# Closing norms with factor and scaled sum in PSUM, and six plain tiles at the head of the second MLP

## The chip, the cores and the metric

The kernel runs on one core of a Trainium2 chip. A core has TensorE (PE, matmuls into PSUM), VectorE (DVE), ScalarE (ACT), GpSimd (POOL) and SyncE (SP), which issues the DMAs here. The metric is the device time of one execution in microseconds. Before the change it is 2682.29 us, the median of 3 runs (2672.32 to 2683.67).

## What is computed

One inference step of a decoder trunk of two layers, for a prompt of 1024 tokens and a sample group of 32, with shared weights, in fp32. Layer 0 mixes by differential attention and a convolution, layer 1 by an S5 state space. Each mixer is followed by an MLP with squared ReLU, and every one of these four stages has an RMS norm before it and one behind it, ahead of the residual sum:

```python
def rms_norm(x, g, eps=RMS_EPS):
    xf = x.astype(jnp.float32)
    y = xf * lax.rsqrt(jnp.mean(xf * xf, axis=-1, keepdims=True) + eps)
    return (y * g.astype(jnp.float32)).astype(x.dtype)

def sq_relu_mlp(xn, w_up, w_down):
    return jnp.square(jax.nn.relu(xn @ w_up)) @ w_down

# D_MODEL = 1024, D_FF = 4096, SEQ = 1024, DEC_BATCH * DEC_SEQ = 32
for l in range(DEPTH):                     # DEPTH = 2
    ...                                    # l = 0: attention + conv mixer, l = 1: S5 mixer
    hp = hp + rms_norm(mix, g_mix_post[l])
    ...
    hp = hp + rms_norm(sq_relu_mlp(rms_norm(hp, g_ffn_pre[l]), w_ffn_up[l], w_ffn_down[l]), g_ffn_post[l])
    hs = hs + rms_norm(sq_relu_mlp(rms_norm(hs, g_ffn_pre[l]), w_ffn_up[l], w_ffn_down[l]), g_ffn_post[l])
```

## The kernel before

The 1056 tokens lie along the columns, in three chunks of 352 (`NCH`, `CH`); the 1024 features are eight tiles of 128 partitions (`KT`). Each operand of a large matmul is split into a high and a low part, and a product is three matmuls, hi x hi, hi x lo, lo x hi (`mm3`, L203 to L205). A plain group, one weight tile against one chunk, is therefore 24 matmuls of 352 columns in one tile of PSUM. PSUM tiles come from one pool of eight with a single tag (`PS`); SBUF tiles of 128x352 come from another (`H`). A weight tile of 128x1024 is loaded (`wraw`), cast on ScalarE (`whi`, L196), and its rest taken on VectorE (`wlo`, L197).

A stage ends in `posts`: per chunk, the products of the last weight tiles are added up in `y`, squared (ScalarE, L300) and summed over the eight tiles into `ssq`, seven additions of which the last (`YV`) is on VectorE and the others on POOL (L301). `colsum` turns `ssq` by one matmul (`cs`, L183) into column sums, and `factor_of` (L175 to L178, ScalarE and VectorE in turn) into the factor `rpost`. Then `post` goes over the eight tiles: L323 scales `y` in place, L324 subtracts it from the residual `hres` (the tile holds the negative sum; four of eight on POOL, `HP`), `split` makes the next stage's operand (ACT L229, VectorE L230), ScalarE squares, and POOL adds these squares into `ssq2` (L333), from which the next stage's factor comes in the same way. While one chunk's `post` runs, TensorE does the products of the next chunk.

There are four such closings. Three of them (mixer 0, first MLP, mixer 1) lead into a next stage; the fourth, of the second MLP, into the outputs, its last chunk in `end`. The second MLP (`ffn_q`) does its first four units of 128 hidden rows as plain groups (`NB`, `up`), three chunks each, one hidden tile `hp` at a time going out to DRAM (`hid`), and the other 28 in 14 pairs: seven products of 24 matmuls with 264 columns for two units, a Strassen-like scheme. Its operands are sums of halves of the input (`sums`, on VectorE and ScalarE, L460 to L469, in the background) and sums of quarters of two weight tiles (`quads`, tiles `op`, from `wq`), which VectorE and ScalarE split as well (L226, L227). L646 takes a plain group's result out of PSUM, with the ReLU and the factor of the norm.

The order of the instructions on each engine is set by a scheduling framework when the kernel is built: the Python code is written in generators whose yields give rough costs, and the framework places the emitted instructions. Within the engines' order, waits are semaphores. SP's queue keeps the program's order, and a DMA whose source isn't ready holds up what stands behind it.

Of the kernel before, what the change touches and what calls it, by code (L numbers as in the profile page):

```python
# [13 lines left out]
ALU = mybir.AluOpType  # L14
# [8 lines left out]
CH = 352  # L23
NCH = T // CH
# [4 lines left out]
NB = 4  # L29
PW, RT = 7.0, 0.9  # L30
XA = ()
TR = 1.0
HP, YV, PE, EP = (0, 2), (7,), 14.0, ((1, 1), (2, 1))


def chunk(c):
    return slice(c * CH, (c + 1) * CH)
# [13 lines left out]
class Step:  # L51
# [261 lines left out]
    def post(self, y, c, s, gk, l, h, nxt):  # L313

        nc = self.nc
        yield PW
        r = self.H("rpost")
        self.factor_of(r, self.colsum(s, CH))
        s2 = self.H("ssq2") if nxt is not None else None
        yield 0.5  # L320
        for k in range(KT):
            yc = y[k][:, chunk(c)]
            nc.vector.scalar_tensor_tensor(yc, yc, self.g(gk, l, k), r, op0=ALU.mult, op1=ALU.mult)  # L323
            (nc.gpsimd if k % 4 in HP else nc.vector).tensor_sub(yc, h[k], yc)  # L324
            if nxt is not None:
                X, rn, rs, g2, l2 = nxt[:5]
                self.split(X[k][0][:, chunk(c)], X[k][1][:, chunk(c)], yc, self.g(g2, l2, k))
                if k == 0:
                    nc.scalar.activation(s2, yc, AF.Square)
                else:  # L330
                    q = self.H("sq")
                    nc.scalar.activation(q, yc, AF.Square)
                    nc.gpsimd.tensor_add(s2, s2, q)  # L333
            yield 1.0
        if nxt is None:
            yield from self.store(y, c)
            return
        self.fins.append((s2, nxt[1][:, chunk(c)]))
        if c == NCH - 1:
            for k in range(KT):  # L340
                self.dma(nxt[2][k], y[k])
            if nxt[5]:
                self.T = [[None] * 4 for _ in range(4)]
                self.bg_add(self.sums(list(y), g2, l2, self.T), TR)

# [280 lines left out]
    def ffn_q(self, l, X, r, res, nxt, early=None, beside=None):  # L626


        nc = self.nc
# [3 lines left out]
        raws = {}  # L633
        slot = [None, 3]

        def raw(u):
            if u < 32:
                raws[u] = [self.S("wq") for _ in range(2)]
                for i in range(2):
                    self.dma(raws[u][i][:, :1024].rearrange("p (k m) -> p k m", k=4),  # L640
                             up_w[512 * i:512 * i + 512, u * P:(u + 2) * P].rearrange("(k p) m -> p k m", p=P))

        def up(u, c):
            pt = self.block(w[u], slice(0, P), X, c)
            t1 = self.H("t")
            nc.vector.scalar_tensor_tensor(t1, pt, 0.0, r[:, chunk(c)], op0=ALU.max, op1=ALU.mult)  # L646
            if slot[1] == 3:
                slot[:] = self.S("hp"), 0
            h = slot[0][:, chunk(slot[1])]
            slot[1] += 1  # L650
            nc.scalar.activation(h, t1, AF.Square)
            self.dma(hd[u][:, chunk(c)], h)
            self.pump(3.7)
# [4 lines left out]
        ops = []  # L658
        for c in range(NCH):
            self.chunk_ready(c)  # L660
            if c == NCH - 1:
                raw(NB)
                steps = self.quads(raws[NB])
            for u in range(NB):
                up(u, c)
                if c == NCH - 1:
                    del w[u]
                    if u:
                        ops.append(next(steps))
        slot[0] = None  # L670
        self.drain()

# [1 line left out]
        for k in range(4):  # L674
            z = self.T[2][k][:, B:]
# [22 lines left out]
        def ahead():  # L698
            prep(0)
            yield  # L700
            for u in range(4):
                if u == 2:
                    prep(1)
                hload(u)
                yield

        first, more = True, None
        for u in range(NB, 32, 2):
            hu, hv = self.S("hu"), self.S("hv")
            nxt_ops = []  # L710
            if u == 30:
                more = ahead()
            else:
                raw(u + 2)
            nsteps = None
            for p in range(7):
                while len(ops) <= p:
                    ops.append(next(steps))
                wh, wl = ops[p]
                for x in range(2):  # L720
                    xs = slice(264 * x, 264 * x + 264)
                    pt = self.PS("mq")[:, :264]
                    for k in range(4):
                        xh, xl = rhs[p][k]
                        self.mm3(pt, (wh[:, k], wl[:, k]), (xh[:, xs], xl[:, xs]), k == 0, k == 3)
                    c0, c1 = slice(264 * x, 264 * x + 264), slice(B + 264 * x, B + 264 * x + 264)
                    if p == 0:
                        nc.scalar.copy(hu[:, c0], pt)
                    elif p == 1:
                        nc.vector.tensor_add(hu[:, c1], hu[:, c0], pt)  # L730
                    elif p == 2:
                        nc.vector.tensor_add(hu[:, c0], hu[:, c0], pt)
                    elif p == 3:
                        nc.vector.tensor_add(hv[:, c0], hu[:, c1], pt)
                    elif p == 4:
                        nc.vector.tensor_add(hu[:, c1], hu[:, c1], pt)
                        nc.vector.tensor_add(hv[:, c1], hv[:, c0], pt)
                    elif p == 5:
                        nc.vector.tensor_add(hu[:, c1], hu[:, c1], pt)
                    else:  # L740
                        nc.vector.tensor_add(hv[:, c0], hv[:, c0], pt)
                wh = wl = None
                ops[p] = None
                if p == 5:
                    nc.vector.scalar_tensor_tensor(hu, hu, 0.0, r, op0=ALU.max, op1=ALU.mult)
                    nc.scalar.activation(hu, hu, AF.Square)
                    self.dma(hd[u], hu)
                if more is not None:
                    next(more, None)
                elif p >= 0:  # L750
                    if nsteps is None:
                        nsteps = self.quads(raws[u + 2])
                        raws.pop(u, None)
                    nxt_ops.append(next(nsteps))
            nc.vector.scalar_tensor_tensor(hv, hv, 0.0, r, op0=ALU.max, op1=ALU.mult)
            nc.scalar.activation(hv, hv, AF.Square)
            self.dma(hd[u + 1], hv)
            ops, steps = nxt_ops, nsteps
# [9 lines left out]
        for i, (_, f, g, j) in enumerate(seq[:last]):  # L768
# [3 lines left out]
            for m in range(2):  # L772
                k = 2 * j + m
                if f == 0:
                    y[k] = self.S("y")
                for c in range(NCH):
                    pt = self.block(wd[i], slice(m * P, (m + 1) * P), hs, c)
                    yc = y[k][:, chunk(c)]
# [73 lines left out]
LAM = 0.8 - 0.6 * math.exp(-0.3 * 0)  # L852
TH, RC, RE = 20, 1.0, 1.0
KA, SL = 1, 1.0
CV, CN, DL = 0.85, 1.0, 5.0


class Step0(Step):
# [1598 lines left out]
```

## Time and profile before

| | |
|---|---|
| median of 3 runs | 2682.29 us (2672.32 to 2683.67) |
| profiled execution | 2678.91 us |
| its span | 2677.1 us |
| TensorE (PE) busy | 2497.3 us, 93% |
| VectorE (DVE) busy | 1713.5 us, 64% |
| ScalarE (ACT) busy | 1006.0 us, 38% |
| GpSimd (POOL) busy | 754.6 us, 28% |
| mean granted TensorE clock | 0.97 |

The profile records one execution. Busy time is work on the engine, without waiting; 1.8 us of the execution lie outside the span. The stages that follow one another on TensorE meet at about 650 to 735 us (mixer 0 to MLP), 1440 to 1535 (MLP to S5 mixer), 1880 to 1955 (S5 mixer to the second MLP), and the second MLP's plain units end at 1968.

### The profile page before, as it was taken

The page shows a single profiled execution, that of the slowest core. Times are in us where ns is not written, and L with a number is a line of the kernel's source. Part 1 is how long each engine was busy: PE and PEld are TensorE (multiplying, and loading weights), DVE is VectorE, ACT ScalarE, POOL GpSimd, SP SyncE. Part 2 cuts the span into 40 slices and gives each one's busy share as a digit, 9 for nine tenths or more (in the row PEclk, how much of TensorE's full clock was granted, in tenths as well). Part 3 has the DMA queues.
Part 4 walks back from the last instruction along what each step waited for, and adds up shares of the span by engine and source line. Part 5 has one row for each costly group of instructions (what it writes and reads, how often), then busy time and mean ns, then how long its engine had stood idle before and what let it go on. Part 6 is the DMA issues. An engine that isn't in the chain of part 4 may idle for free. (4 is left out here: it accounts for less than half of the span.)

```text
span 2677.1 us, 42789 instructions
## 1 busy us (share of the span) xinstructions
PE 2497.3 (93%) x16349; PEld 2384.9 (89%) x16349; DVE 1713.5 (64%) x3070; ACT 1006.0 (38%) x2022; POOL 754.6 (28%) x1093
## 2 busy tenths in 40 slices
PE   8999969798899999999998888799879999999998
PEld 7999946588899999999998877699779999999997
DVE  6888557746876545555545998851787676455435
ACT  6133446644532122222224566633553333412103
POOL 0211011123408873444204588611510000000004
PEclk9999989999899999999999899899889999999999
DMA  6355499652312223223212533104032333433221
GB/s 188 96 172 169 161 314 324 195 177 81 105 34 79 90 93 72 63 79 103 96 47 69 172 126 126 40 24 127 30 121 97 117 109 129 176 97 108 84 81 66
DMA packets 240580, 310.33 MB, mean 116 GB/s; under 512 B 27572, under 2 KB 168130, under 8 KB 240367
## 3 DMA queue, kind: packets, MB, share of 16 engines
q1 hardware_dynamic: 240043, 307.36, 35.4%
q8 instruction: 129, 2.11, 0.3%
q14 instruction: 76, 0.62, 0.1%
q10 hardware_dynamic: 332, 0.23, 0.0%
HBM read 234.79 MB, written 73.18 MB: 115 GB/s over the span
## 5 line engine op out<-in xcount | busy, mean ns | idle before, releaser
L203 PE MATMUL mm<-hh,whi 128*128 128x352 f32 x1536 | 498.3, 326 | 0.0
L205 PE MATMUL mm<-hh,wlo 128*128 128x352 f32 x1536 | 496.4, 323 | 0.0
L204 PE MATMUL mm<-hl,whi 128*128 128x352 f32 x1536 | 496.3, 323 | 0.0
L203 PE MATMUL mm<-zh,whi 128*128 128x352 f32 x1344 | 449.7, 336 | 2.4 <-DVE u L1836 1.7
L204 PE MATMUL mm<-zl,whi 128*128 128x352 f32 x1344 | 440.5, 328 | 2.9 <-DVE zl L227 2.9
L205 PE MATMUL mm<-zh,wlo 128*128 128x352 f32 x1344 | 440.0, 328 | 0.0
L301 POOL TENSOR_TENSOR ssq<-ssq,sq 128x352 f32<-128x352 f32 x72 | 73.1, 1016 | 920.9 <-ACT sq L300 920.1
L204 PEld LDWEIGHTS mm<-hl,whi 128*128 128x128 f32 x1536 | 289.8, 189 | 0.5 <-issue 0.2
L203 PEld LDWEIGHTS mm<-hh,whi 128*128 128x128 f32 x1536 | 289.2, 189 | 0.6 <-issue 0.2
L205 PEld LDWEIGHTS mm<-hh,wlo 128*128 128x128 f32 x1536 | 289.3, 188 | 0.0
L197 DVE TENSOR_TENSOR wlo<-wraw,whi 128x1024 fp32r<-128x1024 f32 x152 | 193.7, 1278 | 145.6 <-ACT whi L196 142.4
L196 ACT CAST whi<-wraw 128x1024 fp32r<-128x1024 f32 x152 | 158.5, 1047 | 301.0 <-DMA wraw<-in_w_ffn_down 156.5
L203 PEld LDWEIGHTS mm<-zh,whi 128*128 128x128 f32 x1344 | 258.5, 193 | 8.7 <-issue 3.7
L204 PEld LDWEIGHTS mm<-zl,whi 128*128 128x128 f32 x1344 | 258.7, 192 | 6.2 <-DVE zl L227 3.9
L205 PEld LDWEIGHTS mm<-zh,wlo 128*128 128x128 f32 x1344 | 257.9, 192 | 0.1
L605 DVE TENSOR_TENSOR y<-y,mm 128x352 f32<-128x352 f32 x312 | 156.0, 518 | 80.1 <-PE mm L205 78.1
L571 ACT ACTIVATE t<-t 128x352 f32<-128x352 f32 x96 | 47.7, 498 | 318.2 <-DVE t L570 318.2
L203 PE MATMUL mm<-xh,whi 128*128 128x352 f32 x480 | 159.0, 333 | 4.6 <-DVE xr L289 4.6
L782 DVE TENSOR_TENSOR y<-y,mm 128x352 f32<-128x352 f32 x144 | 75.1, 521 | 136.9 <-PE mm L205 136.9
L984 DVE SCALAR_TENSOR_TENSOR acc<-proj,keep,acc 128x1024 f32<-128x1024 f32 x120 | 156.8, 1306 | 3.2
L204 PE MATMUL mm<-xl,whi 128*128 128x352 f32 x480 | 155.8, 326 | 0.0
L205 PE MATMUL mm<-xh,wlo 128*128 128x352 f32 x480 | 155.7, 325 | 0.0
(540 smaller groups left out, 5495.6 us busy)
## 6 DMA issues: line engine op xcount, KB each, us to landing
pg<-in_cache_k SPq DMA_DIRECT2D x128, 256.0 KB
pg<-in_cache_v SPq DMA_DIRECT2D x128, 256.0 KB
wraw<-in_w_ffn_down SPq DMA_DIRECT2D x64, 512.0 KB
wraw<-in_w_ffn_up SPq DMA_DIRECT2D x36, 512.0 KB
hr<-hid SPq DMA_DIRECT2D x32, 528.0 KB
wq<-in_w_ffn_up SPq DMA_DIRECT2D x28, 512.0 KB
hres<-res SPq DMA_DIRECT2D x24, 528.0 KB
res<-y SPq DMA_DIRECT2D x24, 528.0 KB
```

Of the source, the lines that this page charges most:

```text
L196: nc.scalar.copy(hi[:, :n], raw[:, :n])
L197: (eng or nc.vector).tensor_sub(lo[:, :n], raw[:, :n], hi[:, :n])
L203: nc.tensor.matmul(out, wh, xh, start=first, stop=False)
L204: nc.tensor.matmul(out, wh, xl, start=False, stop=False)
L205: nc.tensor.matmul(out, wl, xh, start=False, stop=last)
L301: (nc.vector if k in YV else nc.gpsimd).tensor_add(s, s, q)
L571: nc.scalar.activation(t1, t1, AF.Square)
L605: nc.vector.tensor_add(yc, yc, pt)
L782: nc.vector.tensor_add(yc, yc, pt)
L984: nc.vector.scalar_tensor_tensor(acc[:, :NP], u[:, i:i + NP], w[:, k, i:i + 1], acc[:, :NP], op0=ALU.mult, op1=ALU.add)
```

## The change

Three things. In `post`, the factor `rpost` is written to a PSUM tile instead of an `H` tile; the scaled sum goes to a PSUM tile `ypost` of its own instead of back into `y`; and all eight subtractions are on VectorE, out of that tile (L325 and L326 after the change). Over the kernel, 44 subtractions move from POOL to VectorE. In `ffn_q`, six units instead of four are plain (`N1`), the weights of units 4 and 5 being prepared in the last chunk's loop over the first four; the quarters' sums for the first pair are built beside these two units' six groups, and 13 pairs remain. And `DL`, a number yielded once by the generator of the conv norm, is 14 instead of 5. With that edit alone the instruction order of all five engines stays as it was: the caller steps the generator and drops what it yields.

```diff
@@ -29,8 +29,8 @@
 NB = 4
 PW, RT = 7.0, 0.9
 XA = ()
-TR = 1.0
-HP, YV, PE, EP = (0, 2), (7,), 14.0, ((1, 1), (2, 1))
+TR, N1 = 1.0, 6
+YV, PE, EP = (7,), 14.0, ((1, 1), (2, 1))
 
 
 def chunk(c):
@@ -314,14 +314,16 @@
 
         nc = self.nc
         yield PW
-        r = self.H("rpost")
+
+        r = self.PS("rpost")[:, :CH]
         self.factor_of(r, self.colsum(s, CH))
         s2 = self.H("ssq2") if nxt is not None else None
         yield 0.5
         for k in range(KT):
             yc = y[k][:, chunk(c)]
-            nc.vector.scalar_tensor_tensor(yc, yc, self.g(gk, l, k), r, op0=ALU.mult, op1=ALU.mult)
-            (nc.gpsimd if k % 4 in HP else nc.vector).tensor_sub(yc, h[k], yc)
+            z = self.PS("ypost")[:, :CH]
+            nc.vector.scalar_tensor_tensor(z, yc, self.g(gk, l, k), r, op0=ALU.mult, op1=ALU.mult)
+            nc.vector.tensor_sub(yc, h[k], z)
             if nxt is not None:
                 X, rn, rs, g2, l2 = nxt[:5]
                 self.split(X[k][0][:, chunk(c)], X[k][1][:, chunk(c)], yc, self.g(g2, l2, k))
@@ -659,14 +661,19 @@
         for c in range(NCH):
             self.chunk_ready(c)
             if c == NCH - 1:
-                raw(NB)
-                steps = self.quads(raws[NB])
+                raw(N1)
+                steps = self.quads(raws[N1])
             for u in range(NB):
+                if c == NCH - 1 and NB + u < N1:
+                    w[NB + u] = self.ffn_prep(l, ("u", NB + u))
                 up(u, c)
                 if c == NCH - 1:
                     del w[u]
-                    if u:
-                        ops.append(next(steps))
+        for u in range(NB, N1):
+            for c in range(NCH):
+                up(u, c)
+                ops.append(next(steps))
+            del w[u]
         slot[0] = None
         self.drain()
 
@@ -705,7 +712,7 @@
                 yield
 
         first, more = True, None
-        for u in range(NB, 32, 2):
+        for u in range(N1, 32, 2):
             hu, hv = self.S("hu"), self.S("hv")
             nxt_ops = []
             if u == 30:
@@ -852,7 +859,7 @@
 LAM = 0.8 - 0.6 * math.exp(-0.3 * 0)
 TH, RC, RE = 20, 1.0, 1.0
 KA, SL = 1, 1.0
-CV, CN, DL = 0.85, 1.0, 5.0
+CV, CN, DL = 0.85, 1.0, 14.0
 
 
 class Step0(Step):
```

What this does to the order, at the end of mixer 1. VectorE, the end of chunk 0's closing, before (`gl` is the next operand's low part, `wlo` a weight's, L301 the sum that `cs` of the next chunk waits for):

```order
L230 SCALAR_TENSOR_TENSOR gl_18003<-y_18784,gain_g_mix_post,gh_18002 128x352
L197 TENSOR_TENSOR wlo_19037<-wraw_19036,whi_19039 128x1024
L230 SCALAR_TENSOR_TENSOR gl_18201<-y_18876,gain_g_mix_post,gh_18200 128x352
L230 SCALAR_TENSOR_TENSOR gl_18399<-y_18878,gain_g_mix_post,gh_18398 128x352
L301 TENSOR_TENSOR ssq_19042<-ssq_19042,sq_19208 128x352
```

and after:

```order
L326 TENSOR_TENSOR y_18926<-hres_18931,ypost_19280 128x352
L197 TENSOR_TENSOR wlo_19085<-wraw_19084,whi_19087 128x1024
L230 SCALAR_TENSOR_TENSOR gl_18249<-y_18924,gain_g_mix_post,gh_18248 128x352
L301 TENSOR_TENSOR ssq_19090<-ssq_19090,sq_19261 128x352
L230 SCALAR_TENSOR_TENSOR gl_18354<-y_18925,gain_g_mix_post,gh_18353 128x352
L230 SCALAR_TENSOR_TENSOR gl_18447<-y_18926,gain_g_mix_post,gh_18446 128x352
```

Two of the L230 now stand behind L301. VectorE, chunk 2's closing, where the scalings (eight from the factor on) end, before:

```order
L323 SCALAR_TENSOR_TENSOR y_18877<-y_18877,gain_g_mix_post,rpost_19524 128x352
L323 SCALAR_TENSOR_TENSOR y_18878<-y_18878,gain_g_mix_post,rpost_19524 128x352
L324 TENSOR_TENSOR y_18614<-hres_19232,y_18614 128x352
L324 TENSOR_TENSOR y_18784<-hres_19234,y_18784 128x352
L230 SCALAR_TENSOR_TENSOR gl_17838<-y_18529,gain_g_mix_post,gh_17837 128x352
```

and after, from the factor on:

```order
L178 SCALAR_TENSOR_TENSOR rpost_19588<-rs_t_19591,rpost_19588 128x352
L325 SCALAR_TENSOR_TENSOR ypost_19597<-y_18577,gain_g_mix_post,rpost_19588 128x352
L325 SCALAR_TENSOR_TENSOR ypost_19603<-y_18662,gain_g_mix_post,rpost_19588 128x352
L325 SCALAR_TENSOR_TENSOR ypost_19611<-y_18747,gain_g_mix_post,rpost_19588 128x352
L325 SCALAR_TENSOR_TENSOR ypost_19649<-y_18832,gain_g_mix_post,rpost_19588 128x352
L325 SCALAR_TENSOR_TENSOR ypost_19657<-y_18923,gain_g_mix_post,rpost_19588 128x352
L325 SCALAR_TENSOR_TENSOR ypost_19665<-y_18924,gain_g_mix_post,rpost_19588 128x352
L326 TENSOR_TENSOR y_18577<-hres_19288,ypost_19597 128x352
```

The eight scalings in place with two subtractions behind them have become six scalings into six PSUM tiles and then the subtractions that free these. TensorE at the same place, with the engines that an instruction waits for, before (`mm` are plain groups, `cs` is the column sum of `ssq2` of chunk 1):

```order
L205 MATMUL mm_19552<-gh_18398,wlo_19037 128x352
L183 MATMUL cs_19603<-ssq_2675_19315,ones 128x352 [waits Pool_49]
L203 MATMUL mm_19610<-gh_17837,whi_19021 128x352 [waits Activation_49]
L204 MATMUL mm_19610<-gl_17838,whi_19021 128x352
L205 MATMUL mm_19610<-gh_17837,wlo_19019 128x352
```

and after:

```order
L205 MATMUL mm_19619<-gh_18446,wlo_19085 128x352
L183 MATMUL cs_19673<-ssq_2731_19371,ones 128x352 [waits DVE_49,Pool_49]
L203 MATMUL mm_19680<-gh_17885,whi_19069 128x352 [waits DVE_49]
L204 MATMUL mm_19680<-gl_17886,whi_19069 128x352
L205 MATMUL mm_19680<-gh_17885,wlo_19067 128x352
```

`cs` and the group behind it now wait for VectorE as well; what they wait for are the first two L326 above, which free their PSUM tiles. SP at the end of the second MLP's plain units, before:

```order
L96 DMA hid_19435<-hp_19725 128x352 x2
L96 DMA wq_19779<-in_w_ffn_up 128x4x256
L96 DMA wq_19780<-in_w_ffn_up 128x4x256
L96 DMA hid_19435<-hp_19725 128x352
L96 DMA hid_19435<-hp_19847 128x352 x3
L96 DMA wq_19960<-in_w_ffn_up 128x4x256
L96 DMA wq_19961<-in_w_ffn_up 128x4x256
```

and after:

```order
L96 DMA hid_19499<-hp_19797 128x352 x2
L96 DMA wq_19851<-in_w_ffn_up 128x4x256
L96 DMA wq_19852<-in_w_ffn_up 128x4x256
L96 DMA wraw_19855<-in_w_ffn_up 128x8x128
L96 DMA hid_19499<-hp_19797 128x352
L96 DMA wraw_19898<-in_w_ffn_up 128x8x128
L96 DMA hid_19499<-hp_19931 128x352 x3
```

The two plain weights (`wraw`) stand right behind the first pair's quarters (`wq`) and ahead of the last hidden tiles.

## Rows read from the trace of the kernel before

**Rows 1.** Busy time of TensorE, share of the span, instructions (page, part 1)

```profile
PE 2497.3 (93%) x16349; PEld 2384.9 (89%) x16349; DVE 1713.5 (64%) x3070; ACT 1006.0 (38%) x2022; POOL 754.6 (28%) x1093
```

**Rows 2.** TensorE's waits, 650:735, 1440:1535, 1880:1955: total us, times, longest

```profile
PE cs L183 <- DVE ssq L301: 11.8, 2, 8.3
PE cs L183 <- POOL ssq L333: 3.7, 1, 3.7
...
PE cs L183 <- DVE ssq L301: 15.8, 2, 9.6
...
PE cs L183 <- DVE ssq L301: 12.2, 2, 10.7
PE cs L183 <- POOL ssq L333: 2.0, 1, 2.0
```

**Rows 3.** VectorE's timeline, mixer 1, chunk 1: start us, us, instruction

```profile
1911.37 6.83 DVE L323 SCALAR_TENSOR_TENSOR y<-y,gain_g_mix_post,rpost 128x352 f32<-128x352 f32 x8
...
1919.75 0.57 DVE L230 SCALAR_TENSOR_TENSOR gl<-y,gain_g_mix_post,gh 128x352 fp32r<-128x352 f32 x1
1920.24 0.51 DVE L324 TENSOR_TENSOR y<-hres,y 128x352 f32<-128x352 f32 x1
...
1923.06 5.83 DVE L230 SCALAR_TENSOR_TENSOR gl<-y,gain_g_mix_post,gh 128x352 fp32r<-128x352 f32 x6
1928.82 0.51 DVE L301 TENSOR_TENSOR ssq<-ssq,sq 128x352 f32<-128x352 f32 x1
```

**Rows 4.** TensorE's timeline, first product of the first pair: [idle before]

```profile
1976.08 0.59 PE L203 MATMUL mq<-gh,op 128*128 128x264 f32 x1 [7.75 <-ACT op L226]
```

**Rows 5.** TensorE by stretch: us, busy (instructions), granted clock, DMA share, GB/s

```profile
1842.00:1882.00 40.00, 40.00 (x249) 1.00 0.10 27
...
1976.00:2011.00 35.00, 26.28 (x167) 0.77 0.14 45
2011.00:2051.00 40.00, 40.00 (x331) 1.00 0.31 108
...
1884.00:1920.00 36.00, 25.25 (x137) 0.81 0.13 41
...
694.00:712.00 18.00, 14.44 (x77) 0.91 0.08 32
```

**Rows 6.** VectorE's timeline, mixer 1, chunk 2

```profile
1931.58 1.39 DVE L646 SCALAR_TENSOR_TENSOR t<-mm,r 128x352 f32<-128x352 f32 x3
...
1935.43 6.14 DVE L323 SCALAR_TENSOR_TENSOR y<-y,gain_g_mix_post,rpost 128x352 f32<-128x352 f32 x8
...
1946.44 1.27 DVE L230 SCALAR_TENSOR_TENSOR gl<-y,gain_g_mix_post,gh 128x352 fp32r<-128x352 f32 x1
1947.64 0.51 DVE L646 SCALAR_TENSOR_TENSOR t<-mm,r 128x352 f32<-128x352 f32 x1
```

**Rows 7.** POOL's timeline, the same chunk

```profile
1943.86 8.18 POOL L333 TENSOR_TENSOR ssq<-ssq,sq 128x352 f32<-128x352 f32 x7 [1.47 <-ACT sq L332]
```

**Rows 8.** TensorE's timeline, column sums in chunk 2 of the three closings

```profile
703.67 0.75 PE L183 MATMUL cs<-ssq,ones 128*128 128x352 f32 x2
...
1502.05 0.75 PE L183 MATMUL cs<-ssq,ones 128*128 128x352 f32 x2
...
1929.38 0.86 PE L183 MATMUL cs<-ssq,ones 128*128 128x352 f32 x2 [1.43 <-DVE ssq L301]
...
1933.92 0.75 PE L183 MATMUL cs<-ssq,ones 128*128 128x352 f32 x2
```

**Rows 9.** VectorE's timeline, scalings of chunk 2: mixer 0 (begun), first MLP

```profile
704.28 1.08 DVE L323 SCALAR_TENSOR_TENSOR y<-y,gain_g_mix_post,rpost 128x352 f32<-128x352 f32 x2
...
1498.60 6.12 DVE L323 SCALAR_TENSOR_TENSOR y<-y,gain_g_mix_post,rpost 128x352 f32<-128x352 f32 x8
```

**Rows 10.** TensorE's waits, 2615:2677: total us, times, longest

```profile
PE oT L513 <- DVE y L324: 1.8, 3, 1.2
```

**Rows 11.** SP's queue in order of time: start us, us

```profile
1969.41 1.03 SPq L96 DMA_DIRECT2D wq<-in_w_ffn_up  x2
```

**Rows 12.** VectorE's timeline: low part of the first operand

```profile
1981.02 0.68 DVE L227 TENSOR_TENSOR op<-wq,op 128x512 fp32r<-128x512 f32 x1
```

## The prediction

> **What bounds the kernel now.** I read the page's busy table first: TensorE is busy 93% of the span [rows 1], so only its idle time and its half-speed time can be won. The list of what TensorE waits for, cut to the three stretches where one stage's closing norm runs into the next stage, gives the idle time that the change aims at [rows 2]: 11.8 + 3.7 us at the end of mixer 0, 15.8 at the end of the first MLP, 12.2 + 2.0 at the end of mixer 1, 45.5 us in all. Nearly all of it is the column sum `cs` waiting for `ssq` (L301), whose last addition is on VectorE. In VectorE's timeline of one such closing chunk the reader is to see why it is late: the eight scalings L323 alone take 6.83 us, and from their start at 1911.37 to the end of L301 at 1929.33 lie 18.0 us without a hole [rows 3]. VectorE is the engine that these waits hang on, not TensorE. The other idle time is at the second MLP: TensorE waits 7.75 us for the first combined operand [rows 4], and the seven products of the first pair (168 matmuls) then fill 1976 to 2011 with 26.3 us of work in 35 us [rows 5].
>
> **What a VectorE instruction costs there.** A 128x352 operation whose tensor comes from PSUM goes at 1.39/3 = 0.46 us each (L646) [rows 6]. While POOL runs its seven additions in one piece [rows 7], an L230 (two tensors in SBUF) takes 1.27 us and the L646 right after it, with PSUM source, 0.51 [rows 6]. So an operand in PSUM keeps an operation out of POOL's way. L230 stays as it is: 0.49 us from start to start when POOL rests (1919.75 to the next), 5.76/6 = 0.96 on average [rows 3].
>
> [...]
>
> **The closing norms, chunk by chunk.** Now: 18.0 us = 0.5 (L301) + 7.4 (eight L230) + 10.1 (eight L323 and VectorE's four subtractions). Then: 16 operations of 0.46 = 7.4, plus 7.4, plus 0.5 = 15.3. So 2.6 us less in chunk 1. In chunk 0 the order also puts two L230 behind L301, 1.9 us more; some weight splits stand between, so I take 4 us instead of 4.5. The four subtractions that leave POOL are priced in this, and POOL's own relief is worth nothing, as only its additions are waited for.
> Bounds: writing to PSUM from VectorE is in no row. With L230 at 0.49 throughout, chunk 1 saves 6.1 us and chunk 0 about 7; with all at 1.2, 0.5 and 2.9. I take the average of today, as POOL still has its seven additions per chunk.
>
> **The price: PSUM tiles.** The pool has eight. A closing chunk now holds one for the factor and up to six for scaled sums at once, and in chunk 2 the order puts six (mixers) or four (MLP) L325 ahead of the first L326 that frees one. There TensorE's next `cs` waits for that first subtraction, where before it waited for nothing on VectorE. In mixer 1 TensorE reaches this point at 1933.92, one group after the `cs` at 1929.38 [rows 8]; the scalings start at 1935.43 [rows 6], and 7 x 0.46 = 3.2 later the first tile is free: 1938.6, a new wait of 4.7 us. Queued behind it is TensorE's whole stream. In mixer 0: 704.28 + 3.2 = 707.5 against 703.67, 3.8 us. At the MLP the scalings start at 1498.60, five operations end at 1500.9, and TensorE arrives at 1502.05: nothing, or 1.6 us if that group runs at full speed [rows 8, 9].
>
> By stage: mixer 0: -4.0 on its first wait of 8.3, -2.6 on the second, -3.7 (the last `ssq` of POOL is covered by the new wait), +3.8 = -6.5. First MLP: -4.0 - 2.6 = -6.6. Mixer 1: -4.0 - 1.5 (all that is there) - 2.0 + 4.7 = -2.8. **Together -15.9**; with the bounds of L230, and each wait's own length as the most that can go, -29 to -5.8. The clock I leave as it is: the stretch from 1884 to 1920 ran at 0.81 of full speed, 0.19 x 36 = 6.8 us lost round a wait of 10.7; that of 694 to 712 at 0.91, 1.6 us lost behind a wait of 3.5 [rows 5]. Shorter waits give some back and new ones take it.
> The last norm (two chunks, at the program's end): TensorE waits there 1.8 us for subtractions [rows 10]. I take 0, between -1.8 and +4.7 for a wait on a tile as above.
>
> **The second MLP.** A plain group of 24 matmuls takes 24 x 40/249 = 3.86 us, six of them 23.1; the seven products of a pair take 168 x 40/331 = 20.3 [rows 5]. Trading a pair for two plain units costs 2.8 us of TensorE time, with two plain weights to load and split in place of a pair's two quarters. It buys cover: from the last plain matmul (1976.08 - 7.75 = 1968.3) to the end of the first pair at 2011 now lie 42.7 us for 20.3 us of work. With the change the six groups run in this place. But their weights go into SyncE's queue right behind the two `wq` loads, which went out only at 1969.41, after the last plain group had ended [rows 11], and their low parts stand in VectorE's row behind 22 sums and splits. So TensorE still waits here. I bound the start by the first operand's (1976.08) and by the end of that operand's VectorE split (1981.02 + 0.68) [rows 4, 12]: 7.8 to 13.4 us idle, and take 10. With 3.4 us of half speed behind it (half of the 6.8 above, which hold two waits): 10 + 23.1 + 3.4 = 36.5, 6.2 less than 42.7. The next pair must then find its seven operands ready, and only six are built beside the six groups, so I take **-5**. Ends: weights there at once, 23.1, -19.6; 13.4 + 23.1 + 6.8 = 43.3, +0.6.
>
> **The conv norm** changes nothing: the delay is yielded to a caller that throws the number away, and the instruction order stays the same with this edit alone.
>
> **Sum.** -15.9 - 5 = -20.9. The profiled run took 2678.9 us, 3.4 under the median of the runs shown (2682.3); against the median that is 2661.4, so **2661**. A measurement of this kernel tells some 0.5% (13.4 us) from no change.
>
> **Rivals.**
> More is won (2639): L230 meets no POOL addition, and the weights reach TensorE within 4 us: -29 and 4 + 23.1 + 3.4 - 42.7 = -12.2, and -1.8 at the end, -43. For: POOL loses four subtractions a chunk, and the seven additions, 8.18 us of [rows 7], are shorter without collisions. Against: SyncE's queue at 1969.41.
> It is given back (2677): L230 all at 1.2 and weights at the late end: -5.8 + 0.6 = -5.2. For: eight L230 and seven additions now lie side by side for the whole chunk.
> Slower (2705): tiles run out in every chunk, not only in chunk 2. Three norms of three chunks and the last of two are 11 places; 11 x 4.7 = 51.7 new, against -24.4 (the gains above without the two waits already counted) and -5: +22.3. It decides where TensorE arrives over one group (3.86 us) before VectorE's first subtraction. Against: in chunks 0 and 1 TensorE is waiting for `ssq` anyway, which hides it. For: up to seven of eight tiles are held.
> The change does not do what it says (2682): true of the conv norm; the order shows the other two.
>
> **How the numbers follow.** Forecast (2650 to 2671) 0.48; more won 0.17; given back 0.23; slower 0.10; no effect 0.02. Faster by over 0.5% is under 2668.9: 0.85 of the forecast and all of the first rival, 0.58. Within 0.5%: 0.07 + 0.23 + 0.02 = 0.32. Slower: 0.10. The range 2640 to 2688 leaves out half of the first rival and all of the slower one.
>
> **What would show it.** L325 and L326 near 0.46 us each, none over 0.6; L230 still near 0.96; `cs <- ssq` waits of some 20 us less in the three stretches; a new TensorE wait of 4 to 5 us on L326 in chunk 2 of both mixers; at the second MLP one wait of about 10 us on `whi` or `wlo` in place of several on `op`, and the first pair starting without one. I would be wrong if L325 took 0.8 us, if waits on L326 stood in chunks 0 and 1 too, or if the two units' weights were late by more than 13 us.

## The result and the profile after

The changed kernel takes 2640.34 us (median of 4 runs, 2639.03 to 2641.38), the kernel before beside it 2680.78 (4 runs, 2672.32 to 2683.67): a ratio of 0.986, with a 95% interval of 0.9845 to 0.9875. That is 40 us faster where 21 were forecast. The stated range ends at 2640, 0.34 us below the result: that the total still lies inside it is luck. The profiled execution has a span of 2638.4 us against 2677.1, 38.7 less. I compare the sum of the forecast with this 38.7.

To see where the time went I took seven places that both traces have on TensorE and compared their times. In us, differences to the kernel before, each stage by itself:

| stage (from one place to the next) | forecast | measured |
|---|---|---|
| up to the first `cs` of mixer 0's closing (same order of instructions in both) | 0 | +0.9 |
| mixer 0's closing, to the first `hh` product of the first MLP | -6.5 | -7.6 |
| the first MLP's products | 0 | -0.5 |
| first MLP's closing, to the S5 mixer's first `y` product | -6.6 | -6.8 |
| S5 core | 0 | -1.5 |
| mixer 1's closing, to the end of the first four plain units | -2.8 | -2.9 |
| transition, until units 4 to 7 are done | -5 | -17.4 |
| 12 pairs, second MLP's products, last norm, end | 0 | -2.9 |

The sums of the three closings came out as worked out, their terms less so (below). Nearly all that was missed stands in one row, the transition. What TensorE waited for in the three closings of the changed kernel (the list of waits cut to 640 to 735 us, 1430 to 1535, 1870 to 1955: total us, times, longest), to be held against [rows 2]:

```profile
PE cs L183 <- DVE y L326: 4.5, 1, 4.5
PE mm L203 <- DVE y L326: 3.6, 2, 1.9
PE cs L183 <- DVE ssq L301: 3.1, 1, 3.1
...
PE cs L183 <- DVE ssq L301: 4.9, 1, 4.9
PE mm L203 <- DVE y L326: 3.2, 2, 1.6
...
PE cs L183 <- DVE y L326: 1.3, 1, 1.3
...
PE cs L183 <- DVE ssq L301: 4.1, 1, 4.1
PE cs L183 <- DVE y L326: 2.8, 1, 2.8
PE mm L203 <- ACT whi L196: 1.8, 1, 1.8
```

The waits for `ssq` fell from 45.5 us to 12.1. New are the waits for a PSUM tile, on L326: 8.6 us ahead of `cs`, in chunk 2 of all three closings, and 6.8 us ahead of plain groups. In VectorE's timeline of mixer 1 (chunk 1, then chunk 2), beside [rows 3] and [rows 6]:

```profile
1889.93 2.56 DVE L325 SCALAR_TENSOR_TENSOR ypost<-y,gain_g_mix_post,rpost 128x352 f32<-128x352 f32 x5
1892.40 2.24 DVE L326 TENSOR_TENSOR y<-hres,ypost 128x352 f32<-128x352 f32 x5
...
1902.99 1.26 DVE L301 TENSOR_TENSOR ssq<-ssq,sq 128x352 f32<-128x352 f32 x1
...
1911.24 3.05 DVE L325 SCALAR_TENSOR_TENSOR ypost<-y,gain_g_mix_post,rpost 128x352 f32<-128x352 f32 x6
1914.19 2.67 DVE L326 TENSOR_TENSOR y<-hres,ypost 128x352 f32<-128x352 f32 x6
...
1925.96 0.51 DVE L178 SCALAR_TENSOR_TENSOR r<-rs_t,r 128x352 f32<-128x352 f32 x1
```

From the first scaling to the end of L301 chunk 1 takes 1904.25 - 1889.93 = 14.3 us where it took 18.0; one of the eight L230 now stands behind this L301. Five subtractions take 2.24 us, 0.45 each. In chunk 2 the first tile comes free at 1914.19 + 0.45, and TensorE goes on at 1914.86, 0.2 us later. Its timeline there, and at the transition, beside [rows 8] and [rows 4]:

```profile
1914.86 0.93 PE L183 MATMUL cs<-ssq,ones 128*128 128x352 f32 x1 [2.77 <-DVE y L326]
...
1951.73 0.43 PE L203 MATMUL mm<-gh,whi 128*128 128x352 f32 x1 [1.76 <-ACT whi L196]
...
1975.39 0.29 PE L203 MATMUL mq<-gh,op 128*128 128x264 f32 x1
```

Between the fourth and the fifth plain unit TensorE waits 1.76 us, not the 10 of the forecast, and the first pair begins at 1975.39 without any wait, where 7.75 us stood before. Why the weights were there is in SyncE's queue, beside [rows 11]:

```profile
1941.95 1.07 SPq L96 DMA_DIRECT2D wq<-in_w_ffn_up  x2
1943.11 0.46 SPq L96 DMA_DIRECT2D wraw<-in_w_ffn_up  x1
```

The queue reached the first pair's weights 8.0 us before the last of the four plain units ended (1949.97). In the kernel before it was 1.1 us after (1969.41 against 1968.3). This shift of 9 us is what the forecast left out. TensorE's granted clock in the six added groups is 1.00 (TensorE by stretch, as in [rows 5]):

```profile
1950.00:1976.00 26.00, 24.24 (x149) 1.00 0.18 64
```

The experiments ask what made it, and what in the norms' part did the work.

### The profile page after: what moved, and what is told of

It reads as the page before. It is cut to its first block, busy times and chain, and to the rows that moved or that the text cites. A ratio compares the mean times of both kernels' runs of the same rounds, so it can differ in the third digit from the quotient of the medians.

```text
span 2638.4 us, 42720 instructions
## 1 busy us (share of the span) xinstructions
PE 2492.8 (94%) x16325; PEld 2381.3 (90%) x16325; DVE 1677.3 (64%) x3095; ACT 1000.4 (38%) x2019; POOL 698.2 (26%) x1049
## 5 line engine op out<-in xcount | busy, mean ns | idle before, releaser
L301 POOL TENSOR_TENSOR ssq<-ssq,sq 128x352 f32<-128x352 f32 x72 | 72.9, 1012 | 959.6 <-ACT sq L300 958.7
L196 ACT CAST whi<-wraw 128x1024 fp32r<-128x1024 f32 x154 | 160.6, 1047 | 312.9 <-DMA wraw<-in_w_ffn_down 160.3
```

The lines of the kernel that those rows point to most:

```text
L196: nc.scalar.copy(hi[:, :n], raw[:, :n])
L301: (nc.vector if k in YV else nc.gpsimd).tensor_add(s, s, q)
```

## Experiments

All were timed beside the kernel before, whose median was then 2676 to 2680. For the stages I give two stretches of TensorE's trace. **T** goes from the first `cs` of mixer 1's closing to the moment when units 4 to 7 are done (before 154.0 us, changed kernel 133.7). **M** goes from the first `cs` of mixer 0's closing to the first `hh` product (107.3 and 99.7).

**1 to 3: the two parts apart, and the weights' place in the queue.** The norms alone:

```diff
-        r = self.H("rpost")
+        r = self.PS("rpost")[:, :CH]
...
-            nc.vector.scalar_tensor_tensor(yc, yc, self.g(gk, l, k), r, op0=ALU.mult, op1=ALU.mult)
-            (nc.gpsimd if k % 4 in HP else nc.vector).tensor_sub(yc, h[k], yc)
+            z = self.PS("ypost")[:, :CH]
+            nc.vector.scalar_tensor_tensor(z, yc, self.g(gk, l, k), r, op0=ALU.mult, op1=ALU.mult)
+            nc.vector.tensor_sub(yc, h[k], z)
```

> Before with the norms' part alone (factor and scaled sums in PSUM, all subtractions on VectorE; still four plain units). Theory A, each part has its own gain and the norms also bring SyncE's queue to the first pair's weights some 9 us earlier against the last plain group: the last plain group ends 18 us earlier as in the changed kernel, the first pair's operands come up to 9 us earlier, and the total is 2680.8 less 20 to 29, so 2652 to 2661. Theory B, the transition is a matter of the two added plain units alone: 18 us from the norms and 2 us at the end, nothing at the transition, 2661, and the first operand's wait stays at 7 to 8 us.

Measured: 2649.95 us (2648.23 to 2651.41), ratio 0.9893 (0.9868 to 0.9918). M is 100.2 and T 142.2 us. Of T's 11.8 us, 2.9 lie ahead of the end of the four plain units and 8.9 in the transition, with the scheme of pairs untouched. The first pair's products start at once, and the waits for operands from 1940 to 2000 us (total, times, longest) come to 7.7 us, where four of them made 12.0 + 4.4 = 16.4 before:

```profile
PE mq L205 <- DVE op L227: 4.5, 2, 4.0
PE mq L203 <- ACT op L226: 3.2, 2, 2.1
```

SyncE's queue again reaches the first pair's weights 8.0 us before the last of the four plain units ends (1950.29):

```profile
1942.29 1.08 SPq L96 DMA_DIRECT2D wq<-in_w_ffn_up  x2
```

So the norms' part reaches into the next stage through SyncE's queue. Theory A holds, at the good end of its range and a little beyond.

The six plain units alone, with the old norms:

```diff
-TR = 1.0
+TR, N1 = 1.0, 6
...
+                if c == NCH - 1 and NB + u < N1:
+                    w[NB + u] = self.ffn_prep(l, ("u", NB + u))
...
-        for u in range(NB, 32, 2):
+        for u in range(N1, 32, 2):
```

> Before with the six plain units alone (the norms as they were). Theory A: the two added weights are issued after the last plain group, as the first pair's were before (1969.4 against 1968.3), TensorE waits about 10 us for them, and the total falls by 5 to 6 us, 2675. Theory B: the cover of the 18 added groups... that is of the six groups, is worth its 17 us without the norms, 2664, and TensorE waits under 2 us.

Measured: 2671.48 us (2669.37 to 2672.62), ratio 0.9974 (0.9963 to 0.9986); T is 145.9. TensorE's and SyncE's lines:

```profile
1978.26 0.66 PE L203 MATMUL mm<-gh,whi 128*128 128x352 f32 x1 [9.46 <-ACT whi L196]
```

```profile
1969.86 1.03 SPq L96 DMA_DIRECT2D wq<-in_w_ffn_up  x2
1970.94 0.50 SPq L96 DMA_DIRECT2D wraw<-in_w_ffn_up  x1
```

The wait is 9.46 us and the gain 7 (8.1 in T): with the old norms, the forecast's 10 us was right and its -5 near. Before its cast (`whi`, L196) ScalarE stands idle for 4.79 us until the weight has landed, so the load is late, and not the engine. Theory B falls. In the transition the norms alone gain 8.9 us and the six units alone 8.1; together, in the changed kernel, they gain 17.4.

The same, with the two weights requested one chunk earlier:

```diff
-                if c == NCH - 1 and NB + u < N1:
+                if c == NCH - 2 and NB + u < N1:
```

> Before with six plain units, their two weights requested one chunk earlier in the program; the norms as they were. Theory A (the weights' place in SyncE's queue is what TensorE waits for): the weight of unit 4 is issued some 20 us earlier, the wait of about 10 us of the run with the six units alone goes down to 0 to 3 us, and the total is 8 to 12 us under that run, about 2665. Rival: VectorE, full of sums, is what the first added group waits for (its low part): the total stays within 2 us of that run.

Measured: 2658.76 us (2657.14 to 2665.69), ratio 0.9932 (0.991 to 0.9954), 12.7 under the run before it; T is 136.0. The weight of unit 4 goes out at 1949.32, 21.6 us earlier, as expected; that of unit 5, at 1963.76, 9.2 earlier. The wait on `whi` is gone, and of the operands one wait is left, 1.6 us (TensorE's waits, 1960 to 2020):

```profile
1949.32 0.39 SPq L96 DMA_DIRECT2D wraw<-in_w_ffn_up  x1
...
1963.76 1.16 SPq L96 DMA_DIRECT2D wraw<-in_w_ffn_up  x1
```

```profile
PE mq L203 <- ACT op L226: 1.6, 1, 1.6
```

The time at which the weight leaves is what TensorE waited for; VectorE, full of sums, was not the limit.

**4: how much cover is enough.** Eight plain units (`N1 = 8`, the operands still built once each).

> The changed kernel with eight plain units in place of six (12 pairs). With the transition covered by six, two more plain units cost what six plain groups take over seven products: 23.1 - 20.3 = 2.8 us, so 2643 against 2640.3. Rival: the transition still has waits that more cover hides, 2640 or less.

Measured: 2648.69 us (2640.12 to 2652.03), ratio 0.9882 (0.985 to 0.9914). The spread covers the expectation, and the median is 8 us above the changed kernel. T is 136.0, 2.3 over the changed kernel and near the 2.8 worked out; of the 9.5 us that its profiled span is longer, 4.5 had come up before mixer 1's closing and 2.7 come up behind unit 8, and neither is explained by the edit. No gain from more cover shows; its price is told only roughly.

**5 to 7: what in the norms' part does the work.** All subtractions on VectorE, nothing in PSUM (`HP = ()` in the kernel before):

> Before with all eight subtractions on VectorE and nothing in PSUM: scalings in place, four plain units. Theory P, the operands in PSUM are what shortens a closing chunk: L323 and L324 keep two SBUF operands and meet POOL's additions, the closing of chunk 2 in mixer 1 stays at 17 to 18 us, and the total falls by no more than 8 us, 2671 or more. Theory M, POOL's subtractions were what slowed the scalings: L323 goes at 0.50 us each without PSUM, the closing takes about 15 us as in the run with the norms' part alone, no new wait on PSUM tiles comes up, and the total is that run's 2650 or up to 8 us less.

Measured: 2665.0 us (2661.95 to 2668.85), ratio 0.9946 (0.9926 to 0.9966). M is 103.4, T 149.8. Between the theories: 14 us, half of what the norms' part gives. VectorE's timeline of mixer 1, chunk 1:

```profile
1900.33 4.06 DVE L323 SCALAR_TENSOR_TENSOR y<-y,gain_g_mix_post,rpost 128x352 f32<-128x352 f32 x8
1904.30 3.57 DVE L324 TENSOR_TENSOR y<-hres,y 128x352 f32<-128x352 f32 x8
1907.79 8.89 DVE L230 SCALAR_TENSOR_TENSOR gl<-y,gain_g_mix_post,gh 128x352 fp32r<-128x352 f32 x8
1916.60 0.51 DVE L301 TENSOR_TENSOR ssq<-ssq,sq 128x352 f32<-128x352 f32 x1
```

Scalings take 0.51 us each and subtractions 0.45, all in SBUF: what slowed the scalings before (6.83 us for eight, [rows 3]) was POOL's four subtractions, 1.21 to 1.23 us each in its timeline of before, between 1912.04 and 1919.01, with one addition among them. With them gone POOL is idle for most of the block of scalings and subtractions, from 1899.67 to 1906.36 in its own timeline. But the eight L230 then come in one block beside POOL's additions and take 1.11 each, and the closing takes 16.8 us, against 14.3 with PSUM tiles (of these 2.5 us, the one L230 that stands behind L301 there is a part).

Of the other 14 us, from this kernel to that of run 1, the traces put 3.2 in mixer 0's closing, 3.5 in the first MLP's and 7.6 in T. These 7.6 lie behind the four plain units: up to their end both kernels take the same, 87.3 and 87.8 us from the first `cs`. From `cs` of chunk 2 to the factor `r` of chunk 1 VectorE needs 23.7 us here (24.5 before, 19.0 in the changed kernel), the queue comes to the first pair's weights 0.4 us after the last plain unit, not 8.0 before it, and the waits for the first pair's operands are 14.9 us, not 7.7.

The factor alone in PSUM (`z = yc` in the changed kernel):

> The changed kernel with only the factor in PSUM: the scaling is written back in place in SBUF, all subtractions on VectorE, six plain units. Theory P: the subtractions have two SBUF operands and slow to 0.7 to 1.2 us beside POOL's additions, 3 to 6 us more per chunk against 9 us of waits on PSUM tiles that go: 2645 to 2660. Theory M: the subtractions stand ahead of POOL's additions and take 0.44 to 0.5, and TensorE's waits on L326 (8.6 us on cs) are gone: 2630 to 2637.

Measured: 2648.47 us (2644.54 to 2651.5), ratio 0.9885 (0.9864 to 0.9905). M is 101.9, T 140.6. TensorE waits on L326 nowhere in the closings any more, as expected, but 8.94 us on `whi`, and its waits for `ssq` (27.8 us on VectorE, 5.0 on POOL) are longer than the changed kernel's 12.1:

```profile
1957.34 0.66 PE L203 MATMUL mm<-gh,whi 128*128 128x352 f32 x1 [8.94 <-ACT whi L196]
```

The order on VectorE is again scalings, subtractions, L230. The total lies in theory P's range, but not for its reason: the subtractions take 586 ns on average, neither its 0.7 to 1.2 us nor theory M's 0.44 to 0.5. T is 6.9 us longer than in the changed kernel and the wait on `whi` 7.2, so most of what this kernel loses is again a weight that comes late. What it would take with the two weights requested earlier was not run, so how much the scaled sums in PSUM are worth by themselves stays open.

The odd tiles' scaled sums in PSUM, the even ones' in place:

> The changed kernel with the scaled sums of the odd tiles in PSUM, of the even tiles in place. Four PSUM tiles per chunk instead of eight: TensorE's waits for L326 ahead of cs fall from 8.6 to under 5 us. Theory P: half of the subtractions slow by up to 0.7 us, 3 us a chunk, 2640 to 2650. Theory M: 2632 to 2638.

Measured: 2645.11 us (2644.73 to 2649.91), ratio 0.987 (0.9854 to 0.9887). M is 98.6, T 139.0; the wait on `whi` is 8.2 us, those on L326 ahead of plain groups 6.4, and none is left ahead of `cs`. Inside theory P's range, though over all the subtractions hardly slowed (mean 564 ns, against 512), and L230 neither (959 against 935 ns): the wait on `whi` is 6.5 us longer than the changed kernel's, and the total 4.8. Within this one kernel a PSUM operand can be compared with two in SBUF (shortest, middle and longest, ns):

```profile
L326 DVE TENSOR_TENSOR y<-hres,y x44: 511/518/1253, 657.6 to 2628.6; 128x352 f32<-128x352 f32 x44
L326 DVE TENSOR_TENSOR y<-hres,ypost x44: 506/510/515, 658.5 to 2630.0; 128x352 f32<-128x352 f32 x44
```

**8 to 10: the new waits and the queue.** The even tiles of chunk 2 alone in place:

```diff
-            z = self.PS("ypost")[:, :CH]
+            z = yc if c == NCH - 1 and k % 2 == 0 else self.PS("ypost")[:, :CH]
```

> The changed kernel with the even tiles of chunk 2 alone scaled in place (chunks 0 and 1 as changed). If the waits on PSUM tiles in chunk 2 (4.5, 1.3 and 2.8 us on cs) are what they cost, about half of that and of the half speed behind it comes back: 2632 to 2637. If TensorE's later chunk 2 is what lets SyncE's queue arrive in time for the second MLP's weights, the gain is lost there again: 2638 to 2642, with a wait of 3 to 5 us on whi at the transition instead of 1.8.

Measured: 2640.53 us (2638.16 to 2643.16), ratio 0.9853 (0.9835 to 0.9871), the same as the changed kernel. The four plain units end at 1943.7 us, 6.3 earlier than in the changed kernel. TensorE's timeline then has this:

```profile
1951.76 0.66 PE L203 MATMUL mm<-gh,whi 128*128 128x352 f32 x1 [8.09 <-ACT whi L196]
```

It goes on at 1951.76, where the changed kernel went on at 1951.73. The waits for PSUM tiles in mixer 1 cost nothing in the changed kernel, since the weights would not have been there. The wait came out larger than the 3 to 5 us written down for this case. In mixer 0 the edit gained 3.2 us (M is 96.5), and the first MLP's closing lost 3.3, where the waits on L326 ahead of plain groups are 7.1 us instead of 3.2.

The changed kernel, and the kernel of run 8, with the two weights requested one chunk earlier:

> The changed kernel with the weights of units 4 and 5 requested one chunk earlier. The only wait at its transition is 1.8 us on whi, so no more than 1.8 us can come back: 2638 to 2641. If instead the earlier loads delay what stands behind them in SyncE's queue (the hidden tiles and the first pair's quarters), a wait on op comes up and it is slower, 2643 or more.

Measured: 2639.49 us (2632.41 to 2640.39), ratio 0.9857 (0.9841 to 0.9874). The wait on `whi` is gone, and no wait on `op` came up. The median moved by 0.9 us, less than the spread of these four runs, so no price can be told beyond that it is small.

> The kernel whose even tiles of chunk 2 are scaled in place, with the two weights requested one chunk earlier. Its last plain group of the first four units ended 6 us before the changed kernel's, and then TensorE waited 8.1 us for whi. If the weights' place in SyncE's queue was all of that wait, it falls under 2 us and the total to 2632 to 2635. If VectorE's row is what holds the start, it stays at 2638 to 2641.

Measured: 2636.48 us (2631.36 to 2639.16), ratio 0.9848 (0.9832 to 0.9865), between the two expectations. The wait of 8.1 us is gone, one of 2.1 on `op` has come, and T is 128.7 against 135.0 of run 8. The weights' place in the queue was that wait; of the 8.1 us, 6.3 came back in T and 4 in the total.

**11 and 12: mixed order, few tiles.** The scaled sums in SBUF tiles of the pool of five:

```diff
-            z = self.PS("ypost")[:, :CH]
+            z = self.H("ypost")
```

> The changed kernel with the scaled sums in SBUF tiles of the pool of five instead of PSUM (the factor stays in PSUM). Its order on VectorE goes scaling, subtraction, L230 in turn, tile by tile, and no PSUM tile is held for long. Theory P (an operand in PSUM keeps the subtraction out of POOL's way): the subtractions, now amid POOL's additions with two SBUF operands, take 0.8 us or more on average, the closing of chunk 1 in mixer 1 takes 16 us or more, and the total is 2646 or more. Theory O (what the PSUM tiles bought is the mixed order, so that L230 and POOL's additions begin earlier): subtractions at 0.45 to 0.6, closing 13 to 15 us, and 2636 to 2642, with a late wait on whi of some 8 us.

Measured: 2651.01 us (2644.9 to 2653.05), ratio 0.9896 (0.9877 to 0.9915). M is 103.5, T 136.3. Neither theory holds as written. Amid POOL's additions a subtraction with two SBUF operands can take longer, 1.27 us in this pair of lines from VectorE and POOL; another, at 1908.83, took 0.52 beside an addition of 1.33:

```profile
1906.40 1.27 DVE L326 TENSOR_TENSOR y<-hres,ypost 128x352 f32<-128x352 f32 x1
```

```profile
1906.33 0.96 POOL L335 TENSOR_TENSOR ssq<-ssq,sq 128x352 f32<-128x352 f32 x1 [0.28 <-ACT sq L334]
```

The 88 subtractions take 728 ns on average, against 512 from PSUM. The time from the first scaling to the end of L301 is only 12.0 us in chunk 1 all the same, but it is not the same work: two scalings, two subtractions and three L230 now stand behind L301. L230 fell to 716 ns on average; but the pool of five also holds the squares, VectorE now stands idle 6.4 us ahead of its scalings, mostly until a sum of POOL's is done, and TensorE waits 14.2 us in all for `ssq2` from POOL, which the changed kernel doesn't. A clean test of the order alone it was not.

Three PSUM tiles in turn, and the two weights earlier:

```diff
+        zs = [self.PS("ypost")[:, :CH] for _ in range(3)]
...
-            z = self.PS("ypost")[:, :CH]
+            z = zs[k % 3]
...
-                if c == NCH - 1 and NB + u < N1:
+                if c == NCH - 2 and NB + u < N1:
```

> The changed kernel with three PSUM tiles in turn for the scaled sums instead of eight of their own, and the two weights requested one chunk earlier. The waits on L326 ahead of cs and of the plain groups (17.5 us together in the changed kernel) fall under 8 us, the subtractions keep a PSUM operand and L230 is mixed in: 2628 to 2636. If the three tiles make VectorE wait for itself (a scaling for a subtraction two places ahead), the closings are no shorter and the total stays at 2638 or more.

Measured: **2627.97 us** (2625.16 to 2631.52), ratio 0.9815 (0.9799 to 0.9832): 12 us faster than the changed kernel, 11.5 faster than with the earlier weights alone (run 9), and just past the good end of the first expectation. The list of TensorE's waits, the stretches 640 to 735, 1430 to 1520 and 1855 to 2000 us:

```profile
PE cs L183 <- DVE ssq L301: 3.6, 1, 3.6
PE mm L203 <- DVE y L327: 0.3, 1, 0.3
...
PE cs L183 <- DVE ssq L301: 3.5, 1, 3.5
...
PE mm L203 <- DVE y L327: 1.8, 1, 1.8
...
PE cs L183 <- DVE ssq L301: 3.8, 1, 3.8
```

For the subtraction (L327 here) TensorE waits 2.1 us where it waited 15.4. M is 92.5 and T 124.3, 7.2 and 9.4 under the changed kernel; of T's 9.4 the earlier weights alone gave 3.6 in run 9 (T 130.1). L230 takes 827 ns on average, against 935.

## Why the forecast was right, and where it fell short

**The closings were right in size, in part by luck.** The scalings and subtractions of chunk 1 came out: five scalings take 2.56 us and five subtractions 2.24, 0.51 and 0.45 each (0.46 forecast), the sixteen 7.4 as forecast. Chunk 1 went to 14.3 us, not 15.3, since one L230 stands behind L301, the other seven take 0.81 from start to start, not 0.93, and L301 takes 1.26, not 0.5. The waits for `ssq` fell by 33.4 us where the sum took off 24.4, and the new waits on L326 came to 15.4 where it added 8.5: two misses of 9 and 7 us that cancel.

**The reason given for them was half right.** The step "an operand in PSUM keeps an operation out of POOL's way" was read from one L646. The subtractions bear it out (run 7, within one kernel: 515 ns at most with an operand in PSUM, up to 1253 with two in SBUF; on average 512 ns in the changed kernel against 728 in run 11). But the scalings' 6.83 us came from POOL's four subtractions and go with them, PSUM or not (4.06 us in run 5). The forecast gave this gain to the PSUM operand and put "POOL's own relief" at nothing; moving the subtractions off POOL, without PSUM, carries half of the gain, 14 of 28 us. The other half came with the PSUM tiles, and more than half of that, 7.6 us, by way of SyncE's queue (run 5). The traces show L230 lying between the subtractions there and in one block without them; that the limited number of tiles makes the scheduler mix them is argued from the order, not shown by a run of its own.

**The price in PSUM tiles was real and mostly of the forecast size**: 4.5 (3.8 forecast), 1.3 (0 to 1.6) and 2.8 us (4.7). In mixer 1 the scalings started 3.8 us after `cs`, not 6.1 as in the trace of before. The clock, which the forecast left as it was, added to the 2.8: behind this wait, from 1914.8 to 1921.0, TensorE's granted clock is 0.50, 3.1 us lost. With half of chunk 2 in place (run 8) it waits there for nothing, the clock stays at 1.00, and the plain units end 6.3 us earlier. Waits also stood in chunks 0 and 1, the sign that I named for being wrong, but ahead of plain groups only, 3.6 and 3.2 us in two stages. The rival of a wait in every chunk was far too dear: TensorE was indeed waiting for `ssq` there.

**The transition was mis-sized, -5 for -17.4.** The step that failed is "their weights go into SyncE's queue right behind the two `wq` loads, which went out only at 1969.41, after the last plain group had ended". I took a start time from the trace of before, when another part of the same change moves it. The queue there is held by the stores of hidden tiles, which wait for ScalarE, for L646, and so for VectorE's closing of chunk 2: before, SyncE waits 20.8 us for `hp` between 1933.5 and 1956, and 4.2 us right ahead of the `wq` loads; after, 17.2 us between 1915 and 1929, and 4.1. From `cs` of that chunk to the factor `r` of chunk 1 took 1953.39 + 0.52 - 1929.38 = 24.5 us before and 1925.96 + 0.51 - 1907.46 = 19.0 after; from this factor to the `wq` loads it is 15.5 us in both. TensorE, held by the new wait and its half speed, needed 42.5 instead of 39.0 us to the end of the plain units. 5.5 + 3.5 = 9.0 us is the shift of the queue against TensorE. Of the 10 + 23.1 + 3.4 = 36.5 us that the forecast put from the last of the first four units to the first pair, 1.8 + 23.7 = 25.4 were left: the wait fell by 8.2, and the 3.4 of half speed did not come. The 1.2 us held back for a missing seventh operand were not needed either. Alone, the six units waited 9.46 us and gained 7 (run 2), so the price itself was sound. The total is nearly that of the rival "more is won" (2639). Of its conditions, the early weights came true (-12.2), for a reason that it didn't name; that L230 meets no POOL addition (-29) did not.

**The end** was put at 0, between -1.8 and +4.7. Of the last 2.9 us, 2.5 lie behind the last pair, and 2.3 of these behind the last norm's first column sum; no run took them apart.

**The conv norm** did nothing, as forecast: the order of instructions stands as it was, and no kernel was run for it.

## What to carry to other kernels

When two parts of a change meet in one stage, read no start time of the second from the old trace before asking whether the first part moves it; here the forecast missed 12 us by it, and it was hidden in a DMA queue whose front waits for an engine two steps back. Before moving an operation's operand to another memory to be out of a neighbour's way, see what the neighbour was doing: taking the neighbour's work away gave half of the gain. And hold only as many PSUM tiles as the pipeline needs: three in turn did better than up to six at once, 2628 against 2639 us, both with the earlier weights.

## What I had not expected of the hardware

Writing to PSUM from VectorE cost next to nothing here: a scaling took 583 ns into PSUM and 574 in place in SBUF (medians, runs of the changed kernel and of the factor alone in PSUM). A subtraction took 512 ns on average with a PSUM operand; with two SBUF operands it took from 505 to 1274 (run 11), 1.27 us in the instance above beside an addition on POOL. And the stage ahead of the first closing, whose order of instructions no edit touches, ended between 643.5 and 650.6 us in the profiled executions of this study, so a profile's end says less than its stages do.
